# The end of the FFN: early half rows, one buffer for both norms, three block sums rebuilt

## The chip, the cores and the metric

One core of one Trainium2 chip runs the whole kernel. The metric is the device time of one execution in microseconds (us), taken as the median of several runs. Five engines are named as in the profile: PE (matrix multiply), DVE (vector), ACT (scalar), POOL and SP, whose queue issues most of the transfers.

## The reference

A decoder trunk of two layers over 512 tokens with 1024 features. Each layer is an attention mixer and then a gated FFN, and each of the four has a norm ahead of it and a norm behind it, then the residual sum:

```python
def conv_ffn(h, w_up, conv_w, conv_b, w_down):
    u = causal_dwconv(h @ w_up, conv_w, conv_b)
    gate, up = jnp.split(u, 2, axis=-1)
    return (jax.nn.silu(gate) * up) @ w_down

for i in range(DEPTH):
    h = rms_norm(x, pre_g);   h = mixer(h, ...)           # even: MLA + differential, odd: dilated + stick-breaking
    x = x + rms_norm(h, post_g)
    h = conv_ffn(rms_norm(x, ffn_pre_g[i]), ...)
    x = x + rms_norm(h, ffn_post_g[i])
```

The FFN is 2816 wide, and everything is float32.

## The kernel before

**Matrix products.** A float32 operand is split into two float32r parts, a high one and a low one. ACT makes the high part (a copy that rounds) and DVE the low part (a subtraction). One product is then three matmuls on PE (`mm3`, L237 to L241: high by high, high by low, low by high). Weights come through the class `Weights`: SP loads a raw block of 128x1024 (`wraw`, three buffers), ACT and DVE split it into `wh` and `wl` (five buffers), five units ahead of PE.

**Token tiles.** The 512 tokens are four tiles of 128, always taken in the order 3, 2, 1, 0 (`ORDER`). `X[i]` holds the residual stream of a tile. `residual` (L212) takes the two 512-wide halves of a mixer's or FFN's output for a tile, squares each on ACT with a row sum (L226), multiplies by the gain on DVE (L227), gets the reciprocal root on POOL (`rstd`, L172: one operation that adds, L178 or L180, and a power, L181), and adds to `X[i]` (L231, or L234 for the output). `normalise` (L195) then squares `X[i]` (L188), gets a second reciprocal root, writes the normed rows `xn` (L200), and returns `turn`, which transposes them on PE (L206) and splits them into `xh` and `xl` for the next stage (L170, L171).

**The FFN's two phases.** Phase one makes the gated activations, 22 blocks of them in 11 pairs (`PAIRED`, L396 to L437). Phase two is the down projection, done on block sums and differences of the pairs (seven products of half size in place of eight). It has two passes. In the first (L462 to L470) every pair `k` gives eight products into eight PSUM banks. Four of them belong to partial sums which DVE then adds up as `uu` (L475), one 512-wide half row for each of two groups `s`. In the second pass (L482 to L488) the pairs come again in the order `LATER`, and six of the banks go on accumulating. The activations for that pass lie in wherever there was room: the buffers of `X`, of the gains, of `xl` and of the tag `s`. `split_later` splits them for PE, and that frees the buffer.

**Weights of phase two.** `unit` (L302) loads the two row blocks of a pair and forms block differences on DVE (L288) and a block sum (L291). The sum is needed again in the second pass. For pairs 3 to 10 ACT copies it into `t2` (L316). For pairs 0, 1 and 2 there is no `t2`, and the second pass loads one more row block (`raw(sp, "y", k)`) and computes the sum again (two more DVE operations).

**The end of the FFN.** `X` comes back from DRAM (`spill`, L492), the two gains are loaded (L495, L497), and the last four pairs of the second pass (`TAIL`) run bank by bank: for `s` 0 and then 1 the banks a, b, c are completed in turn. After b, `close` finishes tile 3 (later 1), from bank a and from `uu` minus bank b (L223). After c it finishes tile 2 (later 0), whose first half is `uu` minus bank c and whose second half is `uu` itself. In layer 1 the closing writes the output. In layer 0 it calls `normalise` for the odd mixer, and the transposes are put between the last products (L518) and into the mixer's first ones.

**Order.** A scheduler sets the order of instructions on each engine from the program's order and its own costs; on the chip each engine then works through its list strictly in that order, and so does the SP queue. `chp` is the pool with two buffers of tag `s`: `t` of `residual` and `xn` of `normalise` each take one. In the FFN `sp` is a pool with three buffers of tag `y`.

Of the kernel before, what the change touches and what calls it, by code (L numbers as in the profile page):

```python
# [16 lines left out]
P = 128  # L17
# [14 lines left out]
LATER = (3, 4, 5, 6, 7, 10, 0, 1, 2, 8, 9)  # L32
# [53 lines left out]
def trunk(tc, A, out):  # L86
# [3 lines left out]
    with ExitStack() as top:  # L90
# [82 lines left out]
        def rstd(ms, more=None):  # L173
# [3 lines left out]
            if more is None:  # L177
                POOL.tensor_tensor(v[:, :n], ms, epst[:, :n], ALU.add)  # L178
            else:
                POOL.tensor_scalar(v[:, :n], ms, more, EPS, ALU.add, ALU.add)  # L180
# [31 lines left out]
        def residual(i, parts, g, dst=None):  # L212

            ms = chp.tile([P, 2], F32, tag="ms", name="ms2", bufs=4)
            t = chp.tile([P, D], F32, tag="s", name="t")
            c = 0
            for n, a in enumerate(parts):
                less = None
                if isinstance(a, tuple):
                    a, less = a  # L220
                w = a.shape[1]
                if less is not None:
                    DVE.tensor_tensor(t[:, c:c + w], a, less, ALU.subtract)  # L223
                    a = t[:, c:c + w]
                junk = chp.tile([P, D], BF16, tag="junk", name="junk", bufs=1)
                ACT.activation(junk[:, :w], a, AF.Square, scale=D ** -0.5, accum_out=ms[:, n:n + 1])  # L226
                DVE.tensor_tensor(t[:, c:c + w], a, g[:, c:c + w], ALU.mult)  # L227
                c += w
            r = rstd(ms[:, 0:1], ms[:, 1:2])
# [50 lines left out]
        def down_weights(layer, sp, g_tile):  # L280
# [3 lines left out]
            t2, held = {}, {}  # L284
# [13 lines left out]
            def unit(n):  # L298
                if n < 2 * HF:
# [10 lines left out]
                    else:  # L310
                        b = held.pop(k)
                        if k >= 3:
                            if not t2:
                                t = glob.tile([P, KD, S], F32, tag="xh", name="t2")
                                t2.update({j: t[:, j - 3] for j in range(3, HF)})
                            ACT.copy(t2[k], b[:, lo])  # L316
# [24 lines left out]
        def ffn(layer, xnT, pending, final):  # L341
            with ExitStack() as es:
# [8 lines left out]
                down[layer] = down_weights(layer, sp, g_tile)  # L351
# [26 lines left out]
                def home(key):  # L378

                    if key not in homes:  # L380
                        pool, tag = {"X": (glob, key), "g": (glob, "gain"), "s": (chp, "s"), "x": (glob, "xl")}[key[0]]
                        homes[key] = pool.tile([P, 1024], F32, tag=tag, name="hold", bufs=2 if key[0] in "gs" else 1)
# [98 lines left out]

                for n in range(HF - TAIL):  # L482
# [6 lines left out]
                    if n == 3:  # L489
# [5 lines left out]
                g_post = gain("ffn_post_g", layer)  # L495
                if not final:
                    g_next = gain("od_pre_g", 0)  # L497
# [716 lines left out]
```

## Time and profile before

| | us |
|---|---|
| median of 3 runs | 1202.58 (1202.42 to 1202.62) |
| the profiled execution | 1201.1 |
| its span, first to last instruction | 1199.2 |
| PE busy in the span | 1173.5 (98%) |
| DVE busy | 818.5 (68%) |
| ACT busy | 561.3 (47%) |
| POOL busy | 52.5 (4%) |

The profile is of one execution, 1.5 us under the median. Its busy shares are averages over the whole span; PE's matmuls are pipelined, so that two matmuls that start 0.23 us apart are each listed with 0.39 us. Times within the trace count from the span's start. Layer 0's FFN ends at about 628 us, where the odd mixer's first products are under way, and layer 1's at the end of the span.

### The profile page before, as it was taken

The numbers are of one execution on the slowest core, as the hardware profiler recorded it, in microseconds if no ns is written. First come the engines' busy times: TensorE is split into PE (matmuls) and PEld (weight loads), VectorE is DVE, ScalarE is ACT, GpSimd is POOL, SyncE is SP. The second block draws the span as 40 slices with busy tenths as digits, with TensorE's granted clock in tenths as the row PEclk, the third lists the DMA queues.
The fourth block names the chain that finished last, engine by engine and source line by source line (L and its number), as shares of the span: only waits on it lengthen the run. The fifth ranks groups of instructions, "written<-read, shape, count | busy, mean of one in ns | idle before, by whom it ended". The sixth has DMA issues, their size and how long they took to land.

```text
span 1199.2 us, 15060 instructions
## 1 busy us (share of the span) xinstructions
PE 1173.5 (98%) x5616; PEld 948.6 (79%) x5616; DVE 818.5 (68%) x1414; ACT 561.3 (47%) x944; POOL 52.5 (4%) x123
## 2 busy tenths in 40 slices
PE   8999999999999999999999999999999999999996
PEld 7866866798888888887778777887888888888885
DVE  6677358657766667889873456357486666779896
ACT  5565146446343434455543464346353434344552
POOL 2100002310000000000010000001000000000001
PEclk9999999999999999999999999999999999999998
DMA  7320430033333332356535212131333332324471
GB/s 280 106 79 2 130 123 1 36 127 124 95 99 95 99 97 80 115 158 228 193 106 160 80 37 88 54 105 57 103 108 100 94 100 93 102 83 141 123 263 70
DMA packets 39912, 129.94 MB, mean 108 GB/s; under 512 B 4768, under 2 KB 6432, under 8 KB 39712
## 3 DMA queue, kind: packets, MB, share of 16 engines
q1 hardware_dynamic: 37488, 124.47, 32.6%
q10 hardware_dynamic: 2352, 4.52, 1.1%
q8 instruction: 44, 0.72, 0.3%
q14 instruction: 28, 0.23, 0.1%
HBM read 121.09 MB, written 6.29 MB: 106 GB/s over the span
## 4 chain that ended last, share of the span: by engine, by line
issue 76%; PE 17%; POOL 3%; DVE 1%; DMA 1%; ACT 1%; SPq 0%; POOLq 0%; DVEq 0%; ACTq 0%
POOL rr L181 2%; PE sps L656 2%; PE aqk L239 1%; PE o L680 1%; PE aqk L240 1%; PE aqk L241 1%; PE tpp L551 1%; PE sps L746 1%; PE apt L239 1%; PE apt L241 1%; PE av L239 1%; PE apt L240 1%; POOL rv L180 1%; PE av L240 1%; PE av L241 1%
## 5 line engine op out<-in xcount | busy, mean ns | idle before, releaser
L72 DVE TENSOR_TENSOR wl<-wraw,wh 128x1024 fp32r<-128x1024 f32 (+1 forms) x205 | 248.0, 1218 | 179.4 <-ACT wh L71 178.0
L71 ACT CAST wh<-wraw 128x1024 fp32r<-128x1024 f32 (+1 forms) x205 | 213.0, 1047 | 301.5 <-PE u L240 162.7
L239 PE MATMUL u<-xh,wh 128*128 128x512 f32 (+1 forms) x704 | 270.4, 385 | 0.7 <-ACT xh L170 0.7
L240 PE MATMUL u<-xl,wh 128*128 128x512 f32 (+1 forms) x704 | 270.6, 384 | 0.0
L241 PE MATMUL u<-xh,wl 128*128 128x512 f32 (+1 forms) x704 | 270.4, 384 | 0.0
L239 PEld LDWEIGHTS u<-xh,wh 128*128 128x128 f32 x704 | 132.1, 188 | 25.6 <-ACT xh L170 0.9
L241 PEld LDWEIGHTS u<-xh,wl 128*128 128x128 f32 x704 | 132.2, 188 | 25.1
L240 PEld LDWEIGHTS u<-xl,wh 128*128 128x128 f32 x704 | 132.2, 188 | 24.9
L239 PE MATMUL acc<-wh,gh 128*128 128x512 f32 x248 | 97.0, 391 | 0.0
L240 PE MATMUL acc<-wl,gh 128*128 128x512 f32 x248 | 96.9, 391 | 0.1
L241 PE MATMUL acc<-wh,gl 128*128 128x512 f32 x248 | 96.7, 390 | 0.0
L411 ACT ACTIVATE y<-u,cw 128x512 f32<-128x512 f32 x88 | 67.6, 775 | 0.9 <-PE u L375 0.9
L414 DVE SCALAR_TENSOR_TENSOR y<-u,cw,y 128x510 f32<-128x510 f32 x88 | 65.6, 747 | 2.6
L412 DVE SCALAR_TENSOR_TENSOR y<-u,cw,y 128x511 f32<-128x511 f32 x88 | 65.1, 743 | 1.8 <-ACT y L411 1.8
L416 ACT ACTIVATE y<-y 128x512 f32<-128x512 f32 x44 | 27.8, 631 | 81.4 <-DVE y L414 81.4
L240 PEld LDWEIGHTS acc<-wl,gh 128*128 128x128 f32 x248 | 46.8, 189 | 10.3 <-DVE wl L72 0.7
L239 PEld LDWEIGHTS acc<-wh,gh 128*128 128x128 f32 x248 | 46.9, 189 | 9.8 <-DVE uu L475 0.2
L241 PEld LDWEIGHTS acc<-wh,gl 128*128 128x128 f32 x248 | 46.7, 188 | 9.7
L239 PE MATMUL apt<-xh,wh 128*128 128x512 f32 x128 | 50.7, 396 | 0.0
L240 PE MATMUL apt<-xl,wh 128*128 128x512 f32 x128 | 50.4, 394 | 0.0
L241 PE MATMUL apt<-xh,wl 128*128 128x512 f32 x128 | 50.4, 394 | 0.0
L288 DVE TENSOR_TENSOR wraw<-wraw 128x512 f32<-128x512 f32 x56 | 38.3, 687 | 10.3 <-DMA wraw<-in_ffn_w_down 9.5
(278 smaller groups left out, 1950.0 us busy)
## 6 DMA issues: line engine op xcount, KB each, us to landing
wraw<-in_ffn_w_up SPq DMA_DIRECT2D x88, 512.0 KB, 3.6
wraw<-in_ffn_w_down SPq DMA_DIRECT2D x50, 512.0 KB, 3.9
wraw<-in_od_w_dqk SPq DMA_DIRECT2D x12, 512.0 KB, 3.6
wraw<-in_ffn_w_down SPq DMA_DIRECT2D x22, 256.0 KB, 2.7
wraw<-in_ev_w_dqk SPq DMA_DIRECT2D x8, 512.0 KB, 3.6
wraw<-in_ev_w_out SPq DMA_DIRECT2D x8, 512.0 KB, 3.6
spill<-X SPq DMA_DIRECT2D x8, 512.0 KB, 2.6
X<-spill SPq DMA_DIRECT2D x8, 512.0 KB, 6.3
```

Source lines behind the costliest of these rows:

```text
L71: self.nc.scalar.copy(h[:, :w], raw[:, :w])
L72: self.nc.vector.tensor_tensor(l[:, :w], raw[:, :w], h[:, :w].bitcast(F32), ALU.subtract)
L181: POOL.tensor_tensor(r[:, :n], v[:, :n], mhalf[:, :n], ALU.pow)
L239: PE.matmul(o, lh, rh, start=first, stop=False, skip_group_check=more)
L240: PE.matmul(o, lh, rl, start=False, stop=False, skip_group_check=more)
L241: PE.matmul(o, ll, rh, start=False, stop=last, skip_group_check=more)
L288: DVE.tensor_tensor(o, a, b, ALU.subtract)
L411: ACT.activation(y[:, z], u, AF.Identity, bias=c[:, 3:4], scale=c[:, 2:3])
L412: DVE.scalar_tensor_tensor(y[:, z, 1:], u[:, :S - 1], c[:, 1:2], y[:, z, 1:], ALU.mult, ALU.add)
L414: DVE.scalar_tensor_tensor(y[:, z, 2:], u[:, :S - 2], c[:, 0:1], y[:, z, 2:], ALU.mult, ALU.add)
L416: ACT.activation(y[:, 0], y[:, 0], AF.Silu)
L656: PE.matmul(s_ps[:, :w], mq[h][:, i * P:(i + 1) * P], mk[h][:, :w], start=True, stop=True)
```

## The change

Five things change; `residual`, `normalise`, `rstd`, `close` and `unit` hold them.

- `normalise` may be given the buffer `t` of `residual` and writes `xn` into it, so a token tile has one buffer for both norms, in the FFN and in the two mixers.
- `part_of` is one half of `residual`. For tiles 2 and 0 of the FFN the half that is `uu` alone is squared and scaled within the second pass (at `n == 4`), into buffers of `sp`, and the closing does the other half alone. The gain for it is loaded at `n == 2`, the reload of `X` moves from `n == 3` to `n == 5`.
- `rstd` with two partial sums adds the small constant to the first and then the second, two tensor-tensor operations on POOL in place of one tensor-scalar operation.
- For pairs 0, 1 and 2 the block sum is rebuilt in the first pass from its own split (high plus low) into free room of the buffer of `xl`: one ACT copy and one DVE addition, in place of the second load and two DVE operations later.
- `LATER` begins with 0, 1, 2.

```diff
-LATER = (3, 4, 5, 6, 7, 10, 0, 1, 2, 8, 9)
+LATER = (0, 1, 2, 3, 4, 5, 6, 7, 10, 8, 9)
...
-            if more is None:
-                POOL.tensor_tensor(v[:, :n], ms, epst[:, :n], ALU.add)
-            else:
-                POOL.tensor_scalar(v[:, :n], ms, more, EPS, ALU.add, ALU.add)
+            POOL.tensor_tensor(v[:, :n], ms, epst[:, :n], ALU.add)
+            if more is not None:
+                POOL.tensor_tensor(v[:, :n], v[:, :n], more, ALU.add)
             POOL.tensor_tensor(r[:, :n], v[:, :n], mhalf[:, :n], ALU.pow)
...
-        def normalise(i, g, xnT, tags):
+        def normalise(i, g, xnT, tags, xn=None):
             r = mean_square(X[i][:])
-            xn = chp.tile([P, D], F32, tag="s", name="xn")
+            if xn is None:
+                xn = chp.tile([P, D], F32, tag="s", name="xn")
...
+        def part_of(t, ms, n, a, g):
+            c = slice(n * S, n * S + S)
+            o = t[:, c]
+            if isinstance(a, tuple):
+                DVE.tensor_tensor(o, *a, ALU.subtract)
+                a = o
+            junk = chp.tile([P, D], BF16, tag="junk", name="junk", bufs=1)
+            ACT.activation(junk[:, :S], a, AF.Square, scale=D ** -0.5, accum_out=ms[:, n:n + 1])
+            DVE.tensor_tensor(o, a, g[:, c], ALU.mult)
+
+        def begin(pool=None, tag="s"):
+            return ((pool or chp).tile([P, D], F32, tag=tag, name="t"),
+                    chp.tile([P, 2], F32, tag="ms", name="ms2", bufs=4))
+
+        def residual(i, parts, g, dst=None, at=None):
+            t, ms = at or begin()
+            last = 0 if parts[1] is None else 1
+            for n in (1 - last, last):
+                if parts[n] is not None:
+                    part_of(t, ms, n, parts[n], g)
+            r = rstd(ms[:, 1 - last:2 - last], ms[:, last:last + 1])
             if dst is None:
                 DVE.scalar_tensor_tensor(X[i][:], t[:], r[:, 0:1], X[i][:], ALU.mult, ALU.add)
-                return
+                return t
...
-                    if k in t2:
-                        d = t2[k]
-                    else:
-                        r = raw(sp, "y", k)
-                        d = r[:, lo]
-                        sub(d, d, r[:, hi])
-                        add(d, d, c[:, hi])
+                    d = t2[k]
                     sub(d, d, c[:, lo])
...
+                        if key == "xl":
+                            homes[key] = pool.tile([P, KD, S], F32, tag=tag, name="hold")[:].rearrange("p a b -> p (a b)")
+                            t2.update({j: homes[key][:, 1024 + j * S:1024 + (j + 1) * S] for j in range(3)})
...
+                    if k < 3:
+                        ACT.copy(t2[k], w2[0][:, :S].bitcast(F32))
+                        DVE.tensor_tensor(t2[k], t2[k], w2[1][:, :S].bitcast(F32), ALU.add)
...
+                early_q = []
...
-                    if n == 3:
+                    if n == 2:
+                        g_post = gain("ffn_post_g", layer)
+                        if not final:
+                            g_next = gain("od_pre_g", 0)
+                    if n == 4:
+                        for z in range(2):
+                            early_q.append(begin(sp, "y"))
+                            part_of(*early_q[z], 1, uu[:, z], g_post)
+                    if n == 5:
                         for i in ORDER:
                             X[i] = glob.tile([P, D], F32, tag=f"X{i}", name=f"X{i}")
                             nc.sync.dma_start(X[i][:], spill[i * P:(i + 1) * P, :])
...
-                def close(i, cs):
+                def close(i, cs, at=None):
                     if final:
-                        residual(i, cs, g_post, out)
+                        residual(i, cs, g_post, out, at)
                         return
-                    residual(i, cs, g_post)
-                    turns.append(normalise(i, g_next, nx, "tn"))
+                    turns.append(normalise(i, g_next, nx, "tn", residual(i, cs, g_post, None, at)))
...
-                            close(2 - 2 * s, ((uu[:, s], bk["c", s]), uu[:, s]))
+                            close(2 - 2 * s, ((uu[:, s], bk["c", s]), None), early_q[s])
```

More of the change, by code (lines that the diff above doesn't have):

```diff
@@ L210, in normalise @@
             return turn
[L212 to L229, printed above, removed]
+        def part_of(t, ms, n, a, g):
[17 more added lines that the diff above has]
+            r = rstd(ms[:, 1 - last:2 - last], ms[:, last:last + 1])
             if dst is None:
                 DVE.scalar_tensor_tensor(X[i][:], t[:], r[:, 0:1], X[i][:], ALU.mult, ALU.add)
-                return
+                return t
             for q, c in ((nc.sync, slice(0, S)), (nc.scalar, slice(S, D))):
@@ L277, in row_product, with down_weights @@
                     mm3(acc[half], lh, ll, wh[:, c], wl[:, c], first and n == 0, last and n == len(terms) - 1)
-        def down_weights(layer, sp, g_tile):
+        def down_weights(layer, sp, g_tile, t2):
             src = A["ffn_w_down"][layer]
-            t2, held = {}, {}
+            held = {}
             lo, hi = slice(0, S), slice(S, 2 * S)
@@ L311, in unit @@
                         b = held.pop(k)
+                        if k == 3:
+                            t = glob.tile([P, KD, S], F32, tag="xh", name="t2")
+                            t2.update({j: t[:, j - 3] for j in range(3, HF)})
                         if k >= 3:
-                            if not t2:
-                                t = glob.tile([P, KD, S], F32, tag="xh", name="t2")
-                                t2.update({j: t[:, j - 3] for j in range(3, HF)})
                             ACT.copy(t2[k], b[:, lo])
@@ L350, in ffn @@
                 spill = tc_dram[layer]
-                down[layer] = down_weights(layer, sp, g_tile)
+                t2 = {}
+                down[layer] = down_weights(layer, sp, g_tile, t2)
                 xh, xl = xnT
@@ L799, in chain @@
                 def chain(i, acc):
-                    residual(i, acc, g_post)
-                    return normalise(i, g_next, nx, "nn")
+                    return normalise(i, g_next, nx, "nn", residual(i, acc, g_post))
                 turns = []
@@ L1105, in chain @@
                 def chain(i, acc):
-                    residual(i, acc, g_post)
-                    return normalise(i, g_next, nx, "nn")
+                    return normalise(i, g_next, nx, "nn", residual(i, acc, g_post))
                 return nx, [staggered(attend, project, chain)]
```

6 lines of the change are left out of this document (2 added, 4 removed).

## The prediction

> **What bounds the kernel now.** I read the page first, for the share of each engine, then what PE waited for, then PE's order of time where those waits lie. Two lines of the page:
>
> ```profile
> span 1199.2 us, 15060 instructions
> PE 1173.5 (98%) x5616; PEld 948.6 (79%) x5616; DVE 818.5 (68%) x1414; ACT 561.3 (47%) x944; POOL 52.5 (4%) x123
> ```
>
> PE is busy nearly everywhere, and the change takes no matmul away. It can only win where PE stands still, or after PE's last matmul. The list of waits on PE says how much that is:
>
> ```profile
> PE tp L206 <- DVE xn L200: 7.3, 7, 2.8
> PE acc L239 <- DVE uu L475: 0.2, 1, 0.2
> ```
>
> The transposes of the normed rows are the only large item. In order of time, PE's rows around the end of layer 0's FFN (I call it the hand-over) hold four of those seven waits:
>
> ```profile
> 595.64 0.39 PE L240 MATMUL acc<-gl,gh 128*128 128x512 f32 x1
> 595.87 0.39 PE L241 MATMUL acc<-gh,gl 128*128 128x512 f32 x1
> 599.02 1.97 PE L206 MATMUL tp<-ident,xn 128*128 128x128 f32 x8 [2.76 <-DVE xn L200]
> 609.89 0.63 PE L206 MATMUL tp<-ident,xn 128*128 128x128 f32 x4 [0.31 <-DVE xn L200]
> 618.21 0.63 PE L206 MATMUL tp<-ident,xn 128*128 128x128 f32 x4 [0.88 <-DVE xn L200]
> 626.70 1.29 PE L206 MATMUL tp<-ident,xn 128*128 128x128 f32 x8 [0.85 <-DVE xn L200]
> ```
>
> Matmuls start 0.23 apart, so PE was free at 596.10 and stood until 599.02: 2.9 us. The listed idle time counts from a modelled end 0.16 later; the other three gaps are therefore 0.5, 1.0 and 1.0, together 2.5. The table by stretches adds what the first gap costs afterwards (columns: PE, PEld, DVE, ACT, POOL busy, granted clock, DMA):
>
> ```profile
> core 0: us, PE busy (x) PEld busy (x) DVE busy (x) ACT busy (x) POOL busy (x), PEclk, DMA share, GB/s
> 554.00:572.00 18.00, 17.76 (x77) 13.90 (x76) 17.97 (x28) 10.38 (x15) 0.00 (x0) 1.00 0.83 297
> 600.00:602.40 2.40, 2.40 (x10) 2.06 (x9) 1.62 (x4) 1.89 (x5) 0.00 (x0) 0.55 0.00 0
> 616.00:628.00 12.00, 10.09 (x49) 7.30 (x48) 7.42 (x12) 5.59 (x13) 2.35 (x6) 1.00 0.31 100
> ```
>
> Behind the long gap the clock was 0.55 for 2.4 us, which is 1.1 us lost; the gaps of 1.0 left it at 1.00. So the hand-over costs 2.9 + 2.5 + 1.1 = 6.5 us. The other place is the end of the program, where no PE work is left. The first row of this table also shows DVE full in the second pass.
>
> **Hand-over.** The chain of tile 3 in DVE's and POOL's rows:
>
> ```profile
> 590.54 1.22 DVE L72 TENSOR_TENSOR wl<-wraw,wh 128x1024 fp32r<-128x1024 f32 x1 [0.77 <-ACT wh L71]
> 591.69 0.68 DVE L223 TENSOR_TENSOR t<-uu,acc 128x512 f32<-128x512 f32 x1
> 597.36 0.19 POOL L178 TENSOR_TENSOR rv<-ms,epst 128x1 f32<-128x1 f32 x1 [2.64 <-ACT junk L188]
> 597.63 0.55 POOL L181 TENSOR_TENSOR rr<-rv,mhalf 128x1 f32<-128x1 f32 x1
> 598.21 1.41 DVE L200 SCALAR_TENSOR_TENSOR xn<-X,rr,gain 128x512 f32<-128x512 f32 x2 [2.17 <-POOL rr L181]
> ```
>
> The subtraction of tile 3 (591.69) started the moment DVE was done with a weight split. Its bank had been complete for some time: 30 matmuls of 0.227 lie between that bank's last one and the stop at 596.10, so it was ready at 589.3. The weight split in front is the third one of the next mixer, and its load waits for the buffer of the FFN's last block, so it comes as early as DVE gets through the second pass. What the change does to that pass, with DVE's prices by group:
>
> ```profile
> L288 DVE TENSOR_TENSOR wraw<-wraw 128x512 f32<-128x512 f32 x56 | 38.3, 687 | 10.3 <-DMA wraw<-in_ffn_w_down 9.5
> L316 ACT COPY t<-wraw 128x512 f32<-128x512 f32 x16 | 9.9, 619 | 15.4 <-DVE wraw L291 15.4
> ```
>
> Pairs 0, 1 and 2 needed three such operations each and now one; the two early gain products come in. That is 6 fewer and 2 more of 0.69, or 2.8 us less for an engine that was full, and three loads of 512 KB less. Taking 0.6 from start to start, 2.4 us. So the subtraction can move by 2.3, to where its bank is ready; I take 589.4. The early squares and the three copies (0.62 each) go to ACT, which was busy for 10.38 of 18.00 us: no cost.
>
> From the subtraction to `xn` it took 598.21 - 591.69 = 6.5. In the changed order POOL's early addition for tile 2 stands between tile 3's addition and power, which costs one start to start, 597.63 - 597.36 = 0.27; the cheaper first addition gives back 0.1 (below). So `xn` starts at 589.4 + 6.7 = 596.1, and the transposes 0.8 later (599.02 - 598.21), at 596.9. The order of PE's instructions has them four matmuls earlier than before, so PE comes there at 595.2 and stands 1.7 in place of 2.9. The clock: between 1.0 (no loss) and 2.9 (1.1 lost), I take half of the loss. Saved so far 1.2 + 0.55.
>
> Rule against trace, on its own: the Trainium skill, TensorE: Matmul & The Clock Gate, "What's actually happening", lets the clock fall only after an idle window of about 3.4 us. This trace does not quite agree, for a gap of 2.9 was enough; by the rule a gap of 1.7 keeps the full clock, and the sum would be better by another 0.55.
>
> The later gaps: before, the next tile's subtraction stood on DVE behind the previous tile's `xn`. In the changed order it stands right behind the update of `X`, so that two chains overlap on the waits for POOL. Walking the changed list with the durations above, tile 2's `xn` is there at 602.0 and PE at its transposes at 603.2; tile 1's `xn` at 610.3 and PE at 611.2; tile 0's at 615.7 and PE at about 616.2, a gap of some 0.3. I keep 0.8 for all three, from 2.5: 1.7 saved. One buffer for both norms adds no wait here, since tiles 2 and 0 have their own in `sp`. Hand-over: -3.5 (bounds: -5.9, all but 0.6 of it; -0.5, see the first rival).
>
> **End of the program.** The last closings of layer 1:
>
> ```profile
> 1178.57 0.19 ACT L226 ACTIVATION_READ_ACCUMULATOR junk<-t 128x1 f32 x1
> 1178.79 0.69 DVE L227 TENSOR_TENSOR t<-t,gain 128x512 f32<-128x512 f32 x1 [0.85 <-ACT junk L226]
> 1178.85 0.80 POOL L180 TENSOR_SCALAR rv<-ms 128x1 f32<-128x1 f32 x1 [331.81 <-ACT junk L226]
> 1180.33 1.41 DVE L234 SCALAR_TENSOR_TENSOR t<-t,rr,X 128x512 f32<-128x512 f32 x2 [0.85 <-POOL rr L181]
> 1182.99 0.19 ACT L226 ACTIVATION_READ_ACCUMULATOR junk<-t 128x1 f32 x1
> 1184.03 0.30 POOL L180 TENSOR_SCALAR rv<-ms 128x1 f32<-128x1 f32 x1 [3.73 <-ACT junk L226]
> 1185.01 1.42 DVE L234 SCALAR_TENSOR_TENSOR t<-t,rr,X 128x512 f32<-128x512 f32 x2 [1.11 <-POOL rr L181]
> 1187.70 0.39 PE L241 MATMUL acc<-gh,gl 128*128 128x512 f32 x1
> ```
>
> PE ends at 1188, the program 11 us later: four closings hang one behind the other on DVE. From the end of the square to the last step it is 1180.33 - 1178.76 = 1.57 for tiles 3 and 1, and 1185.01 - 1183.18 = 1.83 for tiles 2 and 0, where POOL first waits for the square of `uu`. That square is now done earlier, which makes all four 1.57. But then POOL's addition falls beside DVE's product, as it does at 1178.85, where it took 0.80 instead of 0.30; only the kind of operation gains (0.19 alone, against 0.30). So 4 x 1.47 = 5.9 for 6.8: -0.9. Bounds: with no gain from the kind -0.5; if the addition ran unhindered, the next step would wait for DVE's own product alone, at about 0.95 each, -3.0.
>
> Rule against trace, on its own: the Trainium skill, SBUF — State Buffer, "Who interferes with whom", says that a DVE instruction with two SBUF inputs blocks a GpSimd instruction that reads SBUF for its whole length. The rows 0.80 and 0.30 agree; by it the new addition is blocked as well, and without it the sum here would be the -3.0.
>
> **What is added.** At the head of the first pass DVE gets two additions ahead of its last read of a bank that PE needs:
>
> ```profile
> 497.16 0.75 DVE L414 SCALAR_TENSOR_TENSOR y<-u,cw,y 128x510 f32<-128x510 f32 x1
> 498.26 0.39 PE L239 MATMUL acc<-wh,gh 128*128 128x512 f32 x1
> ```
>
> The read ended at 497.91, PE wanted the bank at 498.26; with 0.6 in front PE stands 0.25, less one matmul which now goes ahead: 0.05 per layer, 0.1 in all (none, or 0.3 each). At the head of the second pass the loads of the gains now stand in SP's queue ahead of a weight block:
>
> ```profile
> 542.17 5.67 SPq L295 DMA_DIRECT2D wraw<-in_ffn_w_down  x2
> 544.17 0.96 DVE L171 TENSOR_TENSOR gl<-hold,gh 128x768 fp32r<-128x768 f32 x1
> 553.33 0.68 DVE L288 TENSOR_TENSOR t<-t,wraw 128x512 f32<-128x512 f32 x1
> 555.86 0.50 PE L239 MATMUL acc<-gh 128*128 128x512 f32 x1 [0.24 <-DVE uu L475]
> ```
>
> The gains wait for a split at the place of 544.17 and go at 545.1. The block follows at 547.5 (end of the first row, less its own 0.33) and has 5.8 us until DVE subtracts it at 553.33. Behind that, on DVE, are the sums `uu` that PE waits for (0.24 at 555.86), so a late block costs PE one for one. Times from issue to landing:
>
> ```profile
> wraw<-in_ffn_w_down SPq DMA_DIRECT2D x50, 512.0 KB, 3.9
> gain<-in_ffn_post_g SPq DMA_DIRECT2D x2, 512.0 KB, 6.2
> gain<-in_od_pre_g SPq DMA_DIRECT2D x1, 512.0 KB, 7.4
> ```
>
> Two gains and the block are 1.5 MB; at the 297 GB/s of the stretch above that is 5.3 us from 545.1, before 553.33. I charge 0.3 (0 to 5.0, third rival). The two mixers' norms keep PE's order; their POOL additions move by tenths either way: 0. Sum: -3.5 - 0.9 + 0.1 + 0.3 = -4.0 on the profiled 1201.1 (span 1199.2 and 1.9 around it). That execution lies 1.5 under the median of 1202.58, so 1198.6 for the median.
>
> **Rivals.** First: DVE is no earlier at tile 3's subtraction, since the reloads of `X` now stand in front of the last blocks' loads. Then PE comes to the transposes 0.9 earlier and they start no earlier: +1.1 there, -1.7 later. With the end and the additions -1.1: 1201.5. For it: the chain needs a load behind a load. Against: three loads are gone.
>
> Second: POOL's addition slips in ahead of DVE's product, and the clock stays up: -3.0 - 5.4 + 0.1 = -8.3, 1194.3. Against it: the 0.80 at 1178.85.
>
> Third, slower: SP's order at the head of the second pass. If the gains are served first, the block lands at 545.1 + 7.4 + 3.9 = 556.4, 3.1 late, and with one gain in layer 1 (6.2) 1.9 late. DVE, late by 3.1 and full, then loses what it saved for the hand-over (-0.6 instead of -3.5): 3.1 + 1.9 - 0.6 - 0.9 + 0.1 = +3.6, 1206.2. It decides once the block takes over 5.8 us. For it: the gains' landing times; against: the rate of 297.
>
> **How the numbers follow.** Forecast 0.53, first rival 0.17, second 0.12, third 0.18. About 0.2% (2.4 us) is what a measurement of this kernel can tell from no change. Faster by more: 0.50 of the forecast, the second rival, 0.02 of the first: 0.64. Within it: 0.18. Slower: 0.18. The range takes in the second rival's point, the forecast's and the first's bounds and the start of the third: 1194.2 to 1204.0.
>
> **What would show it.** Right: the first wait of the transposes at the hand-over under 2 us, the three later ones under 0.5, a clock over 0.8 behind it; POOL's second addition still near 0.7 beside DVE's product, and the last steps of the closings 1.5 after their squares; no wait of PE on `uu` over 0.5. Wrong: PE idle at the head of the second pass, or the subtraction of tile 3 still behind a weight split two us after its bank is complete.

## The result, and the profile after

The changed kernel takes 1194.2 us (median of 4 runs, 1193.39 to 1194.72) against 1202.6 us before (4 runs, 1202.42 to 1204.44): a ratio of 0.9926, 95% interval 0.9909 to 0.9943. A second measurement beside the kernel before gave 0.9932 (0.9913 to 0.9950). It is faster, as forecast, but by 8.4 us where 4.0 were forecast. Its profiled execution took 1194.5 us, with a span of 1192.7. Two lines of its page:

```profile
span 1192.7 us, 15068 instructions
PE 1171.5 (98%) x5616; PEld 948.5 (80%) x5616; DVE 812.7 (68%) x1408; ACT 564.2 (47%) x950; POOL 57.3 (5%) x139
```

Rows of the list of waits on PE. The row of the normed rows was 7.3 us; they are now written into `t`, except in the first norm of the program, so it is two rows. The row for `uu` is gone, and the wait for the first `xh`, at 11 us, was 2.0:

```profile
PE tp L206 <- DVE t L200: 3.2, 5, 1.4
PE ac L244 <- ACT xh L170: 2.3, 1, 2.3
PE tp L206 <- DVE xn L200: 0.9, 2, 0.6
```

PE's transposes at the hand-over, in order of time:

```profile
596.24 1.32 PE L206 MATMUL tp<-ident,t 128*128 128x128 f32 x8 [1.36 <-DVE t L200]
601.89 0.63 PE L206 MATMUL tp<-ident,t 128*128 128x128 f32 x4 [0.23 <-DVE t L200]
603.75 0.60 PE L206 MATMUL tp<-ident,t 128*128 128x128 f32 x4
610.49 1.29 PE L206 MATMUL tp<-ident,t 128*128 128x128 f32 x8 [0.20 <-DVE t L200]
616.07 0.63 PE L206 MATMUL tp<-ident,t 128*128 128x128 f32 x4 [0.64 <-DVE t L200]
```

The first wait is 1.36 for 2.76, the later ones 0.23, 0.20 and 0.64 for 0.31, 0.88 and 0.85. Tile 0's row, the last, comes at 616.07 for 626.70; most of that is order, for it stands 28 matmuls earlier in PE's list than before. The same stretches as before, by busy time (PE, PEld, DVE, ACT, POOL, then clock and DMA):

```profile
554.00:572.00 18.00, 18.00 (x81) 14.92 (x80) 17.97 (x26) 11.58 (x20) 0.00 (x0) 1.00 0.59 193
600.00:602.40 2.40, 2.17 (x13) 1.58 (x12) 2.02 (x4) 2.40 (x5) 1.48 (x3) 1.00 0.00 0
```

DVE is as full as before in the second pass (17.97), the transfers fell from 297 to 193 GB/s, and PE is no longer short of 0.24 us there. The clock stayed at 1.00 where it was 0.55.

A list of waits misses small stalls, so I also compare the start of the same matmul in PE's order (5616 records in every kernel but one). The stretches are START (to the 61st record), H0 and H1 (40 and 45 records around the head of the second pass in layer 0 and 1), LATE (13 records late in layer 0's second pass), HAND (the hand-over, from the 2787th to the 2931st), END (from the start of the last matmul to the end of the span). HAND holds the same 32 transposes and 112 other matmuls in every kernel, whatever their order, and in the kernel of `b_warm` 24 records more. At 0.2267 us a record H0, LATE and H1 take 9.07, 2.95 and 10.20 without any stall.

| us | START | H0 | LATE | HAND | H1 | END |
|---|---|---|---|---|---|---|
| before, first profile | 16.59 | 9.99 | 3.30 | 37.05 | 10.86 | 11.51 |
| before, second (`b_again`) | 15.54 | 9.40 | 2.95 | 36.70 | 12.63 | 11.50 |
| changed, first | 17.06 | 9.07 | 2.95 | 32.71 | 10.20 | 10.42 |
| changed, second (`a_again`) | 15.42 | 9.07 | 2.95 | 32.79 | 10.20 | 10.43 |

Between the first profiles HAND gives -4.34, the three stretches of the second pass -0.92 - 0.35 - 0.66 = -1.93, END -1.09; START (+0.5) and all that isn't listed give +0.9: the span is 6.5 shorter.

### The profile page after: what moved, and what is told of

It reads as the page before. It is cut to its first block, busy times and chain, and to the rows that moved or that the text cites. A ratio compares the mean times of both kernels' runs of the same rounds, so it can differ in the third digit from the quotient of the medians.

```text
span 1192.7 us, 15068 instructions
## 1 busy us (share of the span) xinstructions
PE 1171.5 (98%) x5616; PEld 948.5 (80%) x5616; DVE 812.7 (68%) x1408; ACT 564.2 (47%) x950; POOL 57.3 (5%) x139
## 5 line engine op out<-in xcount | busy, mean ns | idle before, releaser
L177 POOL TENSOR_TENSOR rv<-ms,epst 128x1 f32<-128x1 f32 x40 | 12.1, 307 | 868.3 <-ACT junk L220 799.5
```

## The experiments

All times are medians; a ratio is to the kernel before on the same chip, with its 95% interval.

**How far one execution may be trusted.** `b_again` and `a_again` are the two kernels, unchanged.

> The kernel before, unchanged, profiled a second time. Its first profiled execution took 1201.1 us, its timed ones 1202.4 to 1204.4. Theory A: the timed executions hold a stall that the profiled one happened to miss, of 1.3 us or more; then a second profile has a good chance of lying at 1202.4 or above, and shows the extra time as stalls or as a second stretch of half clock at the hand-over, where the first gap of 2.9 us stands at the edge of what lowers the clock. Rival B: a profiled execution is simply 1.5 us shorter than a timed one; then it lies at 1201.1 +- 0.3 again, with the same gaps.

> The changed kernel, unchanged, profiled a second time beside the kernel before on the same chip. Theory: its first pass, second pass and hand-over take what they took in its first profile (54.5, 42.2 and 32.7 us for the same stretches of PE's matmuls), since nothing there waits for a transfer any more; a change of up to 1.5 us comes from the first 16 us alone, where the clock falls in some executions: 1193.4 to 1195 us. Rival: the second pass of layer 1 loses up to 2.4 us in some executions as in the second profile of the kernel before: then up to 1196.5.

`b_again`: profiled at 1200.68 us, median 1201.1 (11 runs); against other executions of the same kernel beside it 0.9990 (0.9981 to 0.9999), so 0.1% is not resolved by times. The profile lies in neither expected range: 0.4 under its own median, not 1.5. A second stretch of half clock at the hand-over, as theory A had it, was not there; what differs most between the two profiles is START and H1. START is the clock:

```profile
12.00:15.40 3.40, 2.95 (x12) 2.82 (x12) 3.40 (x6) 2.25 (x5) 0.03 (x1) 0.55 0.58 235
```

That is the first profile of before; in `b_again` the same window has PE's clock at 1.00:

```profile
12.00:15.40 3.40, 3.19 (x17) 2.65 (x18) 3.40 (x6) 2.63 (x5) 0.70 (x2) 1.00 0.61 231
```

H1 lost 2.43 us in `b_again`, in waits that were hardly there in the first profile:

```profile
1141.13 0.50 PE L239 MATMUL acc<-wh,gh 128*128 128x512 f32 x1 [0.81 <-DVE uu L475]
1142.33 0.50 PE L239 MATMUL acc<-wh,gh 128*128 128x512 f32 x1 [0.24 <-DVE uu L475]
1143.52 0.50 PE L239 MATMUL acc<-gh 128*128 128x512 f32 x1 [0.23 <-DVE uu L475]
```

`a_again`: 1194.11 us (6 runs), profile at 1192.79, 0.6 under the range expected; its stretches agree with the first to 0.1 us except START, which is 1.6 shorter without half clock there. Its theory holds in this.

**The rebuilt sums alone.**

> The kernel before with one part of the change alone: the sums of pairs 0, 1 and 2 rebuilt in the first pass, and the second pass starting with these pairs. Theory A: this part is what removes PE's small stalls of the second pass (1.9 us in one profile of the kernel before, 2.8 in the other) and what brings tile 3's subtraction to its bank, so that the first gap at the hand-over shrinks from 2.9 to about 1 us and the clock stays: 1201.5 - 1.9 - 2 - 1.1 = about 1196.5. Theory B: the hand-over gets its gain from the early halves and the overlapped chains, and only the small stalls go here: about 1199.6.

> As the run above, but the second pass keeps its old order, with pairs 3, 4, 5 first. Three loads and six operations of DVE per layer are gone in both. Theory A: the small stalls at the head of the second pass come from the order alone (with pairs 3, 4, 5 first, DVE waits 0.69 us once more for ACT ahead of the sums that PE wants), so they are back, 0.3 to 2.4 us per layer, while the hand-over is as in the run above: 0.7 to 2 us slower than it. Rival B: the loads and operations made the stalls; then it is within 0.4 us of the run above.

> The changed kernel with the old order of the second pass (pairs 3, 4, 5 first). Theory A: the order alone sets the small stalls at the head of the second pass: PE loses 0.3 to 1 us per layer there, 1194.9 to 1196.2. Rival B: within 0.4 us of the changed kernel.

The edit of `o_rebuild34`, on the kernel before, at its core; `o_rebuild` has the new `LATER` too, and `e_order` is the changed kernel with the old one:

```diff
-                    if k in t2:
-                        d = t2[k]
-                    else:
-                        r = raw(sp, "y", k)
...
+                    d = t2[k]
...
+                    if k < 3:
+                        ACT.copy(t2[k], w2[0][:, :S].bitcast(F32))
+                        DVE.tensor_tensor(t2[k], t2[k], w2[1][:, :S].bitcast(F32), ALU.add)
```

`o_rebuild` 1197.68 (0.9962, 0.9947 to 0.9977), `o_rebuild34` 1197.14 (0.9957, 0.9940 to 0.9974), `e_order` 1194.46 (0.9935, 0.9917 to 0.9954). HAND is 34.91 and 34.92, and 32.75 in `e_order`; H0 9.59, 9.07, 9.07; H1 10.68, 10.36, 10.20. The order of the second pass is worth nothing that can be seen: theory A of the last two fell. `o_rebuild` lies between its two theories: the first gap became 1.7 and the clock stayed up, as A had it, but of the 3.1 us that A took for the hand-over 2.0 came. So the rebuilt sums are worth 2.0 us of HAND. PE's transposes in `o_rebuild34`:

```profile
597.19 1.32 PE L206 MATMUL tp<-ident,xn 128*128 128x128 f32 x8 [1.49 <-DVE xn L200]
606.75 1.29 PE L206 MATMUL tp<-ident,xn 128*128 128x128 f32 x8 [1.20 <-DVE xn L200]
615.08 1.29 PE L206 MATMUL tp<-ident,xn 128*128 128x128 f32 x8 [0.64 <-DVE xn L200]
623.84 1.29 PE L206 MATMUL tp<-ident,xn 128*128 128x128 f32 x8 [0.87 <-DVE xn L200]
```

The first wait is short already; the later three, 2.7 together, are not.

**Which part of the rebuilding.** Operations or loads were put back.

> The changed kernel with DVE's old load in the second pass: for the seventh to ninth pair of it, two more operations of 0.6 us each on DVE (a block is added back and subtracted again), six in all per layer, 3.6 us; the three loads that the change took away stay away. Theory: the freed DVE is what brings tile 3's subtraction forward (591.7 to 589.0) and what removed the small stalls of PE in the second pass: the subtraction lies 2 to 3 us later against its bank, the first gap at the hand-over grows by 2 to 3 us and the clock falls behind it, and some of the 0.9 us of small stalls come back: +2.5 to +4 us in all, 1196.7 to 1198.2. Rival: order and early halves did it, and DVE has the room: within 0.7 us of 1194.2.

> The kernel before with the rebuilt sums (old order of the second pass), and with the three loads of 512 KB per layer put back that the rebuilding saves; their data are not used. Theory A: the loads made PE's small stalls in the second pass and kept tile 3's subtraction behind its bank (they stand in the load queue ahead of the weights that follow): the second pass loses 0.5 to 2.5 us per layer again, the hand-over goes from 34.9 back to 36.7 or more: 1200 to 1202. Rival B: DVE's operations did; then it stays within 0.5 us of the kernel with the rebuilt sums, 1197.1.

> The kernel before with the rebuilt sums (old order of the second pass), and with the two operations of 0.6 us for each of pairs 0, 1 and 2 put back on DVE (a block added and subtracted again); the loads stay away. In DVE's order the split of the next mixer's third block then stands ahead of tile 3's subtraction again, as in the kernel before. Theory A (operations): the subtraction comes 2 to 3 us after its bank again, the hand-over goes from 34.9 to 36.7 or more, with the clock down behind the first gap: 1199 to 1200. Rival B (loads): within 0.5 us of 1197.1.

> The kernel before with the rebuilt sums (old order of the second pass), and with both put back per layer: the three loads of 512 KB and, behind each, two operations of DVE on what was loaded, as the kernel before has them; only their result is not used. Theory A: a load that DVE has to wait for is what did it (DVE stands 0.8 us at such a load in the kernel before, and everything behind it in DVE's order is late): the hand-over goes from 34.9 back to 36.7 or more, small stalls of 0.3 us or more per layer are back: 1199 to 1202. Rival B: it was neither, but the place of the sums (DVE ahead in the first pass): within 0.6 us of 1197.1 to 1198.0, the three kernels with the rebuilt sums so far.

```diff
                     sub(d, d, c[:, lo])                  # e_dveload, on the changed kernel
+                    if 6 <= n // 2 <= 8:
+                        add(d, d, c[:, lo])
+                        sub(d, d, c[:, lo])
...
+                    if k < 3:                            # the others on o_rebuild34:
+                        r = raw(sp, "y", k)              # o_loads: this line alone
+                        sub(r[:, lo], r[:, lo], r[:, hi])     # o_both: these two as well
+                        add(r[:, lo], r[:, lo], c[:, hi])
                     d = t2[k]
...
+                    if k < 3:                            # o_ops, behind d = t2[k]
+                        sub(d, d, c[:, hi])
+                        add(d, d, c[:, hi])
```

`e_dveload` 1194.42 (0.9938, 0.9925 to 0.9952): HAND 33.16, all else as in the changed kernel; the expected 2.5 to 4 us did not come. In DVE's order the split of the next mixer's third block had moved behind tile 3's subtraction there, so `o_ops` was made to have it in front: 1197.98 (0.9962, 0.9947 to 0.9976), HAND 34.89, though 36.7 was expected of the operations. `o_loads` 1197.45 (0.9961, 0.9948 to 0.9973), HAND 34.87. Neither alone does it. Both together bring back 1.4 of the 2.0: `o_both` 1198.85 (0.9967, 0.9951 to 0.9984), HAND 36.26 where 36.7 was expected. By the times alone `o_rebuild34`, `o_loads`, `o_ops` and `o_both` can't be told apart, so the reading rests on HAND of one profile each. The profiled execution of `o_both` took 1203.0, since it also lost 3.4 us to half clock in the first mixer (last section), and its rows stand later by that. ACT's cast of the third block and DVE's rows:

```profile
591.46 1.05 ACT L71 CAST wh<-wraw 128x1024 fp32r<-128x1024 f32 x1 [1.09 <-DMA wraw<-in_od_w_v]
592.55 1.23 DVE L72 TENSOR_TENSOR wl<-wraw,wh 128x1024 fp32r<-128x1024 f32 x1 [0.81 <-ACT wh L71]
593.69 0.68 DVE L223 TENSOR_TENSOR t<-uu,acc 128x512 f32<-128x512 f32 x1
```

In `o_ops` the split stands in front too, but its block is there, and DVE does not wait:

```profile
586.99 1.05 ACT L71 CAST wh<-wraw 128x1024 fp32r<-128x1024 f32 x1 [0.56 <-DMA wraw<-in_od_w_v]
588.16 1.21 DVE L72 TENSOR_TENSOR wl<-wraw,wh 128x1024 fp32r<-128x1024 f32 x1
589.30 0.68 DVE L223 TENSOR_TENSOR t<-uu,acc 128x512 f32<-128x512 f32 x1
```

So the loss needs a late third block and DVE's order with its split in front of the subtraction. `o_ops` takes the first away. `e_dveload` takes the second away: its block was late too (ACT's cast ended at 588.5, the subtraction had started at 587.6), but the split stands behind, and the first wait stayed at 1.4; it has the rest of the change as well, so this is the weaker of the two. What the lateness costs in `o_both` is clock. PE's listed waits for the four tiles' transposes are 2.14, none, 1.00 and 0.83 in `o_both` and 1.70, 0.62, 0.87 and 0.79 in `o_ops`, 4.0 us in both. The 1.4 by which HAND differs is that PE ran at half clock behind the wait of 2.14, and not behind that of 1.70.

The small stalls are another matter: `o_both` has H0 9.07 and H1 10.65. Over the profiles without the rebuilt sums (before twice, `b_place`, `b_warm`) H0 lost 0.92, 0.33, 0.70, 1.23 and H1 0.66, 2.43, 2.28, 0.74; over the 14 with them H0 lost 0.52 once and else nothing above 0.05, H1 0 to 0.62, 0.24 on the mean. What DVE waits for in layer 1's first pass, 1076 to 1142 us, in `b_again` and then in the changed kernel:

```profile
DVE wraw L288 <- DMA wraw<-in_ffn_w_down: 4.7, 3, 2.2
```

```profile
DVE wraw L293 <- DMA wraw<-in_ffn_w_down: 1.9, 2, 1.5
```

DVE's additions for the new sums, and the split of a held block that now comes early in DVE's order, stand where DVE waited for loads. That this is how the small stalls went is a reading of the rows, which no run tested. That they go with the rebuilt sums, all but the amounts above, whatever loads and operations are put back, is shown.

**The placement of the loads.**

> The kernel before with nothing but the placement: the gains' loads ahead of the fourth block of the second pass, the loads of the rows of X two blocks later. Theory A: the rows' loads (2 MB, in the queue ahead of the last weight blocks) were what made weights late in the second pass and the third block of the next mixer late at the hand-over; then small stalls and the first gap shrink: 2 us or more under the kernel before. Rival B: the placement does nothing by itself: within 0.7 us of the kernel before.

> The kernel before with the rebuilt sums (old order), and with the loads of the gains and of the rows of X placed as in the changed kernel. Theory A: the placement is worth most of the 2.2 us by which the hand-over of the changed kernel is shorter than with the rebuilt sums alone (34.9 to 32.7), since fewer transfers lie ahead of the next mixer's weights: 33.5 or less, about 1196. Rival B: the overlapped chains are worth it (one buffer for both norms, the early halves, the cheaper addition): 34.5 to 35.0 and 1197.1 to 1197.6.

```diff
+                    if n == 2:
+                        g_post = gain("ffn_post_g", layer)
+                        if not final:
+                            g_next = gain("od_pre_g", 0)
-                    if n == 3:
+                    if n == 5:
                         for i in ORDER:
...
-                g_post = gain("ffn_post_g", layer)
```

`b_place` 1203.15 (0.9991, 0.9980 to 1.0001), HAND 37.27, H1 12.48; `o_place` 1198.21 (0.9955, 0.9941 to 0.9970), HAND 34.85. Rival B holds both times by HAND (the time of `o_place` is 0.6 over its range): the placement is worth nothing by itself.

**The overlapped chains.** Three parts were taken out of the changed kernel one by one.

> The changed kernel, but the half rows of uu are squared and scaled in the closing of their tile again. Theory: the early halves are what shortens the closings of tiles 2 and 0 (DVE is rid of one product of 0.6 us, POOL of the wait for a second square): the two closings at the end of the program cost 0.4 to 0.7 more each, and the chains of tiles 2 and 0 at the hand-over as much, of which about half shows on PE: +1.5 to +2.5 us over the changed kernel's 1194.2, that is 1195.7 to 1196.7. Rival: the freed DVE (three pairs rebuilt) does it all, and the early halves are hidden: within 0.5 us of 1194.2.

> The changed kernel, but the second norm at the hand-over takes a buffer of its own again, instead of the first norm's. Theory: no tile waits for a buffer there (two buffers go round, and each is free some us before it is asked for again), so it costs nothing: within 0.3 us of 1194.2. Rival: the row xn of a later tile then waits until the transposes of the tile before it are done, and PE's later gaps at the hand-over grow by 0.5 us or more, 1194.7 and above.

> The changed kernel with the old form of POOL's addition in a closing (one operation that adds the second square and the constant, in place of an early addition and one of the second square). Theory: it is 0.80 beside DVE's product against 0.63 to 0.69 now, so a closing takes 0.1 to 0.2 us longer: 0.4 to 0.7 at the end of the program and as much at the hand-over at most: 1194.5 to 1195.3. Rival: the early additions stand in POOL's queue ahead of a power that the chain waits for, and cost what they save: 1193.8 to 1194.4.

```diff
-                    if n == 4:                                   # e_noearly
-                        for z in range(2):
-                            early_q.append(begin(sp, "y"))
-                            part_of(*early_q[z], 1, uu[:, z], g_post)
...
-                            close(2 - 2 * s, ((uu[:, s], bk["c", s]), None), early_q[s])
+                            close(2 - 2 * s, ((uu[:, s], bk["c", s]), uu[:, s]))
...
-         turns.append(normalise(..., residual(i, cs, g_post, None, at)))            # e_ownbuf
+         turns.append(normalise(..., residual(i, cs, g_post, None, at) and None))
...
-                POOL.tensor_tensor(v[:, :n], v[:, :n], more, ALU.add)               # e_rstd
+                POOL.tensor_scalar(v[:, :n], ms, more, EPS, ALU.add, ALU.add)  # for both additions
```

| | us, ratio | HAND | END |
|---|---|---|---|
| changed | 1194.11, 0.9932 | 32.79 | 10.43 |
| `e_noearly` | 1195.32, 0.9946 (0.9934 to 0.9959) | 33.05 | 11.09 |
| `e_ownbuf` | 1195.01, 0.9947 (0.9935 to 0.9960) | 33.57 | 10.42 |
| `e_rstd` | 1194.74, 0.9924 (0.9902 to 0.9946) | 33.29 | 10.97 |

By the times none of the three can be told from the changed kernel; what follows is read from HAND and END of one profile each, in which the two profiles of the changed kernel agree to 0.1. The early halves are worth 0.66 at the end and 0.3 at the hand-over, 1.0 where 1.5 to 2.5 were expected. POOL's cheaper form is worth 0.55 and 0.5 (all of it in the first wait of the transposes, 1.94 for 1.36), as its theory had it: the old one takes 0.79 in every closing at the end of `e_rstd`, where the new one takes 0.63 to 0.69.

```profile
1173.53 0.79 POOL L180 TENSOR_SCALAR rv<-ms 128x1 f32<-128x1 f32 x1 [331.75 <-ACT junk L221]
1177.93 0.79 POOL L180 TENSOR_SCALAR rv<-ms 128x1 f32<-128x1 f32 x1 [2.96 <-ACT junk L221]
```

The shared buffer, costed at nothing, is worth 0.8 at the hand-over: in `e_ownbuf` the waits of the transposes are 1.54, 0.69, 0.50 and 0.85. Its rival's time came (1194.7 and above), but no row there names a buffer, as the rival has it; DVE's and PE's order differ, and tile 1's update of `X` comes at 607.93 for 605.26, its `xn` behind it alone. These three and the rebuilt sums add up to 2.0 + 0.3 + 0.8 + 0.5 = 3.6 of the 4.1 us of HAND (mean of two profiles each); 0.5 is not assigned. One part was added to the kernel before and three were taken from the changed one, so the sum is a guide only.

**The clock behind the first gap.**

> The kernel before with 12 small matmuls of PE, whose result is thrown away, in the first gap of the hand-over (they wait for the updated rows of tile 3 and fill about 2 us ahead of the first transposes; the transposes stand 7 matmuls earlier in PE's order than before, which those matmuls then follow). Theory A: the clock falls behind a gap of 2.9 us, which costs 1.1 us at half clock; with the gap filled it stays up and the hand-over takes 35.8 us in place of 36.9. Rival B: the half clock is hidden, since DVE's chain for tile 2 sets the pace behind the first gap; then the next gap of PE grows by what the clock gives, and the hand-over takes 36.9 as before.

```diff
                     tp = bank(tags[n], "tp", 4, P)
+                    if fill and n == 0:
+                        for _ in range(12):
+                            PE.matmul(tp[:, 0], ident[:], X[i][:, :P], start=True, stop=True)
...
-                            turns.pop(0)()
+                            turns.pop(0)(fill=m == "a")
```

1203.78 (1.0012, 1.0000 to 1.0025). Each of the 12 leaves two records; the clock was 1.00 from 596 to 602 us, and the hand-over did not get shorter:

```profile
596.57 2.94 PE L207 MATMUL tp<-X,ident 128*128 128x128 f32 x24 [1.02 <-DVE X L234]
599.50 1.32 PE L209 MATMUL tp<-ident,xn 128*128 128x128 f32 x8
607.74 1.29 PE L209 MATMUL tp<-ident,xn 128*128 128x128 f32 x8 [2.80 <-DVE xn L200]
617.99 1.29 PE L209 MATMUL tp<-ident,xn 128*128 128x128 f32 x8 [0.30 <-DVE xn L200]
626.72 1.29 PE L209 MATMUL tp<-ident,xn 128*128 128x128 f32 x8 [0.83 <-DVE xn L200]
```

The next wait grew from 0.31 to 2.80. From the last matmul ahead of the fill to the end of HAND it took 38.9 us, for 37.3 before: neither A's gain nor B's same time. PE's order was not that of before (the four tiles' transposes stand 6, 23, 13 and 11 matmuls earlier), so the clock's price is not isolated. In this order a half clock would have been hidden, since PE waits 2.80 for DVE's chain anyway.

In the order of before it was not hidden whole. `o_ops` has the order of before in DVE's rows of this stretch and no half clock there. ACT's second cast of tile 3's transposes and DVE's product for tile 2, before and in `o_ops`:

```profile
601.02 0.59 ACT L170 CAST xh<-tp 128x512 fp32r<-128x512 f32 x1 [0.27 <-PE tp L206]
602.26 0.69 DVE L227 TENSOR_TENSOR t<-t,gain 128x512 f32<-128x512 f32 x1 [0.78 <-ACT junk L226]
```

```profile
598.58 0.57 ACT L170 CAST xh<-tp 128x512 fp32r<-128x512 f32 x1
598.96 0.68 DVE L227 TENSOR_TENSOR t<-t,gain 128x512 f32<-128x512 f32 x1
```

Before, the transposes ran at half clock, ACT waited for them, its square for tile 2 came behind that, and DVE waited for the square. From tile 3's row `xn` to tile 2's it took 609.00 - 598.21 = 10.79 us, in `o_ops` 605.68 - 595.83 = 9.85. ACT has the square ahead of the second cast in `o_ops`, so how much of the 0.9 is the clock and how much is ACT's order is not separated.

**A version that follows from POOL's rows.**

> The changed kernel, but in a closing the difference uu - bank is written into the bank itself instead of the tile, so that DVE's product with the gain doesn't overwrite what ACT squares: it runs beside the square instead of behind it, and POOL's addition of the second square no longer falls beside that product. In the changed kernel 2.94 us pass from a closing's subtraction to its last step; expected 2.4 to 2.5: four times 0.5 at the end of the program, and some of the 0.36 and 0.39 gaps at the hand-over: -2.0 to -2.6 us, 1191.5 to 1192.2. Rival: reading the bank makes the square or the product slower by what is won, or the order of DVE puts the product behind something else: within 0.5 us of 1194.1.

```diff
-                DVE.tensor_tensor(o, *a, ALU.subtract)
-                a = o
+                DVE.tensor_tensor(a[1], *a, ALU.subtract)
+                a = a[1]
```

1192.36 us (4 runs, 1192.11 to 1192.91; 0.9919, 0.9897 to 0.9940). END is 8.48 for 10.43. DVE's and POOL's rows of a closing in the changed kernel, then in `e_bank`:

```profile
1171.83 0.69 DVE L217 TENSOR_TENSOR t<-uu,acc 128x512 f32<-128x512 f32 x1 [1.25 <-PE acc L246]
1173.37 0.69 DVE L221 TENSOR_TENSOR t<-t,gain 128x512 f32<-128x512 f32 x1 [0.85 <-ACT junk L220]
1173.48 0.63 POOL L179 TENSOR_TENSOR rv<-rv,ms 128x1 f32<-128x1 f32 x1 [3.21 <-ACT junk L220]
1174.77 1.42 DVE L239 SCALAR_TENSOR_TENSOR t<-t,rr,X 128x512 f32<-128x512 f32 x2 [0.71 <-POOL rr L180]
```

```profile
1171.88 0.69 DVE L217 TENSOR_TENSOR acc<-uu,acc 128x512 f32<-128x512 f32 x1 [1.25 <-PE acc L246]
1173.38 0.69 DVE L221 TENSOR_TENSOR t<-acc,gain 128x512 f32<-128x512 f32 x1 [0.81 <-ACT junk L220]
1173.49 0.19 POOL L179 TENSOR_TENSOR rv<-rv,ms 128x1 f32<-128x1 f32 x1 [3.18 <-ACT junk L220]
1174.35 1.42 DVE L239 SCALAR_TENSOR_TENSOR t<-t,rr,X 128x512 f32<-128x512 f32 x2 [0.27 <-POOL rr L180]
```

The product still waits for the square (0.81), so half of the reasoning fell. The gain is the other half: the product has one operand in a bank now, and POOL's addition beside it takes 0.19 in place of 0.63. HAND stayed at 32.71, where some gain was expected. By the times alone `e_bank` and the changed kernel overlap; by END it is 1.9 us better, a little less than the 2.0 to 2.6 expected.

## Why the prediction was right and wrong

**Hand-over, forecast -3.5, measured -4.34 (-4.1 on the mean of two profiles): right in kind, with its terms mis-sized.** Tile 3's subtraction started at 589.02 (forecast 589.4), its row `xn` at 595.43 (596.1), the transposes at 596.24 (596.9), and the first wait was 1.36 (1.7). Tile 2's row started at 601.00, with its second half at 602.80 (602.0), tile 1's at 609.59 (610.3), tile 0's at 615.17 (615.7). The reason given for the first, fewer operations on a full DVE, was half of it: fewer operations or fewer loads would each have done (`o_ops`, `o_loads`). With the prediction's 0.16 added to each listed wait, the first gap went from 2.9 to 1.5, 1.4 less for a forecast of 1.2. The three later ones went from 2.5 to 1.6, 1.0 less for 1.7, and the last of them, listed at 0.64, missed the sign of under 0.5; the other signs of being right came. The clock's loss was put too low. Half clock reached from 598.8 to 602.2 (clock 0.50), and PE worked from 599.02 on, so some 1.6 us were lost and not 1.1; all of it went, and 0.55 was booked. "One buffer adds no wait" was true and missed that it takes 0.8 away.

**End of the program, forecast -0.9, measured -1.09: right.** POOL's addition stayed beside DVE's product, at 0.63 to 0.69, and the last step comes 1174.77 - 1173.33 = 1.44 after the square. The bound of -3.0, for an addition unhindered, is what `e_bank` reaches: 11.51 - 8.48 = 3.03.

**Head of the first pass, forecast +0.1: right, if small**; 240 records of it take 54.53 for 54.40 in layer 0 and 54.56 for 54.40 in layer 1.

**Head of the second pass, forecast +0.3, measured -1.93 (-2.4 on the mean): wrong, and this is the step that failed.** The gains ahead of a weight block in the queue cost nothing. And the prediction quoted PE's 0.24 us wait for `uu`, saw DVE full there, and booked no gain for it. The term should have been a saving of about 2 us. The list of waits showed 0.2 of the 1.9 us lost in that execution and 1.3 of the 2.8 in `b_again`, since it counts from modelled ends and keeps the larger stalls only. The runs show that these stalls go with the rebuilt sums; by which steps is only read from the rows.

**The reference execution.** The sum was made against a profile of 1201.1 and moved up by 1.5 to a median of three runs. In four later measurements the kernel before had medians of 1201.8 to 1203.7 with single runs from 1199.5 to 1206.4; START and H1 are what moved between two profiles. The changed kernel's profiled execution lay 0.3 above its median, not 1.5 below it: 1.8 of the 8.4 us is this, and it is luck. The rest of the miss, 6.6 - 4.0, is the second pass (2.2), HAND (0.8) and END (0.2), less 0.7 lost in START, by chance too, and between.

The rivals: the third (a late weight block) and the first (a subtraction no earlier) did not happen. The second's time, 1194.3, is near the measured one, but not by its mechanism: POOL's addition did not slip in ahead of the product, 1.93 of the 6.5 us of span lie in the second pass, for which it had nothing, and its -5.4 for the hand-over, which the prediction does not work out, is more than came.

## What to carry to other kernels

Where an engine in front of PE is full, its lateness shows on PE as many stalls too small for a list of waits; compare the starts of the same matmul in two traces, or with the bare pace, before a stage is called free. A chain over several engines can hide what PE gains or loses between its links, the clock included, or hand it on where a link waits for PE; so a stage that ends with such chains is priced along the chain, in the order in which each engine works. And before a forecast is tied to one execution, ask which of its stretches would come out otherwise in the next.

## What the runs showed of the hardware

Half clock came in stretches of one length: 3.4 us behind the hand-over's gap in the profiles of before, `b_again`, `b_place` and `o_both`; as long at the start, in some executions of one kernel and not in others; and twice that, once, in the first mixer. `b_place` at the hand-over, and `o_both` in the mixer, where PE had waited 0.79 and 0.90 us:

```profile
600.00:603.40 3.40, 3.40 (x11) 2.83 (x12) 2.81 (x5) 2.85 (x6) 0.00 (x0) 0.50 0.00 0
```

```profile
172.00:179.00 7.00, 7.00 (x15) 3.66 (x15) 3.80 (x9) 2.47 (x6) 0.00 (x0) 0.51 0.69 210
```

The Trainium skill, TensorE: Matmul & The Clock Gate, "What's actually happening", has a free-running window of about 3.4 us, whose place varies against the kernel. The length agrees, and so does the chance in START. That an idle window must pass before a fall does not agree: a listed wait of 2.14 us at the hand-over was enough in `o_both`, while one of 1.94 in `e_rstd` left the clock at 1.00. No run tells whether the length of the wait decides, or where in a window it falls:

```profile
601.02 0.66 PE L206 MATMUL tp<-ident,xn 128*128 128x128 f32 x4 [2.14 <-DVE xn L200]
```

```profile
595.80 1.32 PE L207 MATMUL tp<-ident,t 128*128 128x128 f32 x8 [1.94 <-DVE t L201]
```

At the end of the program POOL's addition of the second square took 0.63 to 0.69 beside a DVE product with two SBUF operands and 0.19 beside the same product with one operand in a bank. The Trainium skill, SBUF — State Buffer, "Who interferes with whom", has DVE and GpSimd share one pair of ports under an exclusive lock; the rows agree, and `e_bank` is a way out of it. A product of DVE did not start while ACT read the same bank (0.81 to 0.82 of waiting in every closing of `e_bank`); whether the chip or the kernel's own waits set that was not tried.
